# Sparse attention's scores with the queries' low parts on half of the array's rows, and six tiles of the merge's linear part computed beside it

## The chip, the cores and the metric

The kernel runs on one core of a Trainium2 chip. That core has TensorE (PE, with its weight loads shown apart as PEld), VectorE (DVE), ScalarE (ACT), GpSimd (POOL), and SyncE (SP), which here only issues transfers. The metric is the device time of one execution in microseconds, lower is better.

## The reference

A decoder layer on 1024 tokens of width 1024 in float32. It has two token mixers, native sparse attention and gated linear attention (GLA), a gated merge of the two, an output projection and a gated feed-forward part. The change touches the scores of two of the three attention branches:

```python
q_pos = lax.dynamic_slice_in_dim(q_rot, s, Q_BLOCK, axis=3) * scale          # 128 queries, head size 64
ss = jnp.einsum('bghqd,bgqnld->bghqnl', q_pos, ks, preferred_element_type=jnp.float32)   # selected blocks
p_s = masked_softmax(ss, m_s)
sw = jnp.einsum('bghqd,bgkd->bghqk', q_pos, kwin, preferred_element_type=jnp.float32)    # window of 512
p_w = masked_softmax(sw, m_w)
return gt[..., 0:1] * o_c + gt[..., 1:2] * o_s + gt[..., 2:3] * o_w
```

and where one product of the merge is computed (`merged = gate_a * (o_a @ w_up_nsa) + gate_b * (o_b @ w_up_gla)`): the GLA half, `o_b @ w_up_gla`, does not depend on the attention.

## The kernel before

**Precision.** TensorE multiplies float32 operands here as `fp32r`, which keeps a shortened mantissa. So nearly every operand is split into a high and a low part (`hi = x` rounded by ACT, `lo = x - hi` by DVE or POOL), and a product is three matmuls: hi·hi, hi·lo, lo·hi.

**Scores.** A head has 64 dimensions, the array 128 rows. The key tile `ks[br][g]` (`key_job`, `br` 0 for selected blocks and 1 for the window, `g` the key group) holds the keys' high part on the 64 rows of its group and the low part on the other 64. The query tile `qs[par]` (`unit`, one per group g and block i of 128 queries) holds in slot 0 the queries' high part on both halves of the rows, in slot 1 their low part on both halves. So one matmul of 128 rows with slot 0 (L1055 in `products`) gives hi·hi + hi·lo, and a second one with slot 1 (L1056) gives lo·hi and also lo·lo. Small bf16 matmuls of 128 columns add the masks: `mdb` on the diagonal block (L1060), `meb` on the window's far block (L1058).

**Groups of scores.** A unit (g, i) covers four heads, as pairs j = 0, 1 with heads `par` 0 and 1. For branch 1 (selected) the row of scores has w = 128·(i+1) columns, for branch 2 (window) at most 640. Up to 512 columns, `pair_scores` does both heads of a pair as one group. Beyond that, `head_scores` does one head as a group, in two parts of at most 512 columns. Over 2 key groups, 8 blocks and 2 pairs this makes 32 pair groups and 64 head groups, 96 in all. After the scores of a group DVE takes the maximum, ACT the exponential, and `weigh` multiplies by gate/sum; then PE transposes the weights (L1133), ACT and DVE split them (`pth`, `ptl`), and PE multiplies by the values (L1142).

**What sets the order on PE.** PE's order is the program's order. In the attention stage the class `Plan` writes it: it keeps a clock of its own with a cost for each step, and when no step of the attention is ready soon it takes a matmul from a queue of filler work (`fill`): gate products of the merge (`gate_job`, tiles `hh`, `hl`), and at the end the products `up_job` (tiles `obh`, `obl`), which are the GLA half of the merge for the last NU = 4 of 8 output tiles; their results go to memory (`ud`) and are read back in the merge. What the plan has not used is run in one piece when it ends (`fill.flush`). The merge (`merge_job`) then does 48 matmuls for an output tile that still needs both halves and 24 for one whose GLA half is done. The orders of the other engines come from a scheduler that works on priorities and on the free buffers of each pool.

**Buffers.** The pool tag "c" (`big`) has NBIG = 18 buffers of 4 KB a partition, for keys, queries, value tiles and many others; a new tile waits until one is free. The GLA state `st` and the zero-padded queries `QZ` have tiles of their own in the pool `mcst`.

**A step that is not changed but matters below.** `gla_diag` (L826) multiplies, for each of 8 chunks, `d["k"][r, j, :]` by `d["q"][r, j, :]` with r the rows 0 to 63 and then 64 to 127, into two different banks. It is the only step before the change in which products use one half of the rows and then the other.

Of the kernel before, what the change touches and what calls it, by code (L numbers as in the profile page):

```python
# [10 lines left out]
F32 = mybir.dt.float32  # L11
F32R = mybir.dt.float32r
BF = mybir.dt.bfloat16
U8 = mybir.dt.uint8
AF = mybir.ActivationFunctionType
OP = mybir.AluOpType
# [82 lines left out]

PAIR, PMAX, PREP = 4, 3, 3  # L100
LAT, WAIT, LOADED = 155.0, 300.0, 1500.0
NBIG, NMID, NSMALL = 18, 10, 8
SCRATCH = 2048
NU, FINE, NGATE = 4, 3, 2


class Plan:
# [52 lines left out]
    def score(self):  # L160
        b, fn, n = self.scores.popleft()
        fn()
        w = 64 if b.br == 0 else 128 * b.nkb
        if b.br == 0:
            cost = 540.0
        else:
            cost = n * (2 * max(107.0, w / 2.4) + 55.0 * (1 + (b.br == 2 and b.i >= 4)))
        self.t += cost
        self.s.pop(0)
        pf = self.p.pop(0) if b.br else 0.0  # L170
        m = n if b.br else 4
# [68 lines left out]
def layer_kernel(ctx, tc, a, outT):  # L240
    nc = tc.nc
    V, S, P, PE, SP = nc.vector, nc.scalar, nc.gpsimd, nc.tensor, nc.sync
    cst = ctx.enter_context(tc.tile_pool(name="cst", bufs=1))

    edge = ctx.enter_context(tc.tile_pool(name="edge", bufs=1, side="right"))
# [4 lines left out]
    mcst = tc.alloc_tile_pool(name="mcst", bufs=1)  # L250
# [14 lines left out]
    def bank(tag, n=512):  # L265
        return banks["pool"].tile([128, n], F32, name=tag, bufs=banks["tags"][tag])
# [30 lines left out]
    def mid(nm, dt=F32, shape=(512,)):  # L297
        return cur["pool"].tile([128, *shape], dt, name=nm, tag=cur["tag"], bufs=cur["bufs"])
# [96 lines left out]
    def products(getw, bank, xh, xl, w0, evac, fine=False):  # L395

        st, out, n = {}, [], len(xh)

        def at(k, i):
            if k + i == 0:  # L400
                st["p"] = bank()
            wh, wl = getw(w0 + k)
            w, x = ((wh, xh[k]), (wh, xl[k]), (wl, xh[k]))[i]
            PE.matmul(st["p"], w, x, start=k + i == 0, stop=k == n - 1 and i == 2)  # L404
            if k == n - 1 and i == 2:
                evac(st["p"])
# [127 lines left out]
    dst = [x[hf][:, i, :] for x, i in ((qg, 0), (qg, 1), (kg, 0)) for hf in range(2)]  # L534
# [121 lines left out]
    swap = list(range(32))  # L656
    for i in range(8):
        swap[i], swap[8 + i] = 8 + i, i
    ks = [[None, None], [None, None]]

    def key_job(br):
        def evac(p, hf):
            if hf == 0:
                ks[br] = [big(f"ks{br}{g}", F32R) for g in range(NG)]
            rc, rs = mid("rc"), mid("rs")
            SP.dma_start(rc, a["rope"][:, 0, hs(hf)])
            SP.dma_start(rs, a["rope"][:, 1, hs(hf)])
            kt, sw = mid("krt"), mid("ksw")
            scaled(kt, p, hf)
            V.stream_shuffle(sw, kt, swap)  # L670
            V.tensor_mul(kt, kt, rc)
            V.tensor_mul(sw, sw, rs)
            V.tensor_add(kt, kt, sw)
            for g in range(NG):
                r, o = slice(64 * g, 64 * g + 64), slice(64 - 64 * g, 128 - 64 * g)
                k = ks[br][g]
                S.activation(k[r, hs(hf)], kt[r, :], AF.Copy)
                V.tensor_tensor(k[o, hs(hf)], kt[r, :], f(k[r, hs(hf)]), OP.subtract)
        return a["w_t"][6 + br], proj(evac)

# [75 lines left out]
        log_sigmoid(lsg[p].rearrange("p a b -> p (a b)"), z)  # L756


    st = [[mcst.tile([128, 256], F32, name=f"st{i}{j}") for j in range(2)] for i in range(2)]
    for i in range(2):  # L760
        for j in range(2):
            P.memset(st[i][j], 0.0)
    obd = dr.tile([128, GH, T], F32, name="obd")
    ob2 = dr.tile([128, GH, T], F32, name="ob2")
    CH = {}

    QZ = [mcst.tile([128, 2, 2, 128], F32, name=f"qz{i}") for i in range(2)]
    for t in QZ:
        P.memset(t, 0.0)

    def gla_prep(c):
        d = CH[c] = {}
# [187 lines left out]
    for n, (h, hf) in enumerate(pieces):  # L960
# [4 lines left out]
        ps = ps_t()  # L965
# [4 lines left out]
        t = tz[:, 0, :]  # L970
# [15 lines left out]
    UN = {}  # L986
# [22 lines left out]
    class Branch:  # L1009
# [34 lines left out]
            if self.i == 0:  # L1044
                V.tensor_mul(p, p, cmul[:, None, :].to_broadcast([128, 4, 64]))

        def products(self, par, s, w, parts):
            d = UN[self.g, self.i]
            kk = ks[self.br - 1][self.g]
            edge = self.br == 2 and self.i >= 4  # L1050
            for o, n in parts:
                dst = s[:, o:o + n]
                kv = kk[:, 128 * self.k0 + o:128 * self.k0 + o + n]
                end = o + n == w
                PE.matmul(dst, d["qs"][par][:, 0, self.j, :], kv, start=True, stop=False)  # L1055
                PE.matmul(dst, d["qs"][par][:, 1, self.j, :], kv, start=False, stop=not end and not (edge and o == 0))  # L1056
                if edge and o == 0:
                    PE.matmul(s[:, 0:128], identb, meb, start=False, stop=not end)  # L1058
                if end:
                    PE.matmul(s[:, w - 128:w], identb, mdb, start=False, stop=True)  # L1060

        def weigh(self, pars, ps, z):

            n = len(pars)
            r, h = tiny("rr", 2, 6)[:, :n], 2 * self.j + pars[0]
            V.reciprocal(r, z[:, :n])
            V.tensor_mul(r, r, UN[self.g, self.i]["gt"][:, self.br, h:h + n])
            for i, par in enumerate(pars):
                p = self.p[par] = ps[i]
                if par:  # L1070
                    S.activation(p, p, AF.Copy, scale=r[:, i:i + 1])
                else:
                    V.tensor_scalar(p, p, r[:, i:i + 1], None, op0=OP.mult)

        def pair_scores(self):

            w = 128 * self.nkb
            s = ps_s().rearrange("p (h n) -> p h n", h=2)[:, :, :w]
            for par in range(2):
                self.products(par, s[:, par, :], w, [(0, w)])  # L1080
            nm, z = tiny("nm", 2, 6), tiny("z", 2, 6)
            V.tensor_reduce(nm, s, AX, OP.max, negate=True)
            p = prob("p", shape=(2, 512))[:, :, :w]
            for par in range(2):
                S.activation(p[:, par, :], s[:, par, :], AF.Exp, bias=nm[:, par:par + 1],
                             accum_out=z[:, par:par + 1])
            self.weigh((0, 1), [p[:, 0, :], p[:, 1, :]], z)

        def head_scores(self, par):
            w = 128 * self.nkb  # L1090
            c = w if w <= 512 else 128 * ((self.nkb + 1) // 2)
            s = ps_s()[:, 512 - c:512 - c + w]
            self.products(par, s, w, [(0, c), (c, w - c)][:1 if c == w else 2])
            nm, z = tiny("nm", 2, 6)[:, :1], tiny("z", 2, 6)[:, :1]
            V.tensor_reduce(nm, s, AX, OP.max, negate=True)
            p = prob("p")[:, :w]
            S.activation(p, s, AF.Exp, bias=nm, accum_out=z)
            self.weigh((par,), [p], z)
# [512 lines left out]
    ready, ps = deque(), {}  # L1611
# [25 lines left out]
    with tc.manual_schedule(engines={mybir.EngineType.SP}):  # L1637
# [6 lines left out]
        for i, (n, p, *h) in enumerate(todo):  # L1644
# [93 lines left out]
```

## Time and profile before

| | us |
|---|---|
| median of three timed runs (1650.31 to 1654.77) | 1653.8 |
| the profiled execution | 1651.47 |
| its span, first to last instruction | 1649.6 |
| PE busy | 1583.9 (96%) |
| DVE busy | 1070.0 (65%) |
| ACT busy | 809.7 (49%) |
| POOL busy | 752.0 (46%) |
| mean granted TensorE clock | 0.99 |

The span is 1.9 us shorter than the execution's time, and that time is 2.3 us below the median of the timed runs. In the trace the attention stage runs from about 395 us (first scores at 396.8) to 812 us (last product with values), the rest of the filler to 819, the merge to 886. A matmul's row in the timeline gives its start and a modelled length that overlaps the next one's, so what a matmul costs on a full PE is the distance from its start to the next start. If its weights were not yet loaded when it started, its row is longer by that time. A PEld row is the load of the stationary operand; "64\*128" in a row is the array area used, 64 rows by 128 columns.

### The profile page before, as it was taken

How to read it: one execution, taken by the hardware profiler on the slowest of the kernel's cores; microseconds unless marked ns; L12 is line 12 of the kernel's file. 1: busy time of each engine (PE TensorE's matmuls, PEld its weight loads, DVE VectorE, ACT ScalarE, POOL GpSimd, SP SyncE). 2: the span in 40 equal slices, each digit the busy share in tenths (PEclk: the TensorE clock that was granted, in tenths of full speed). 3: DMA queues.
4: the chain of work that ended last, by engine and by line, in shares of the span. 5: the costliest groups of instructions: out<-in, count | busy, mean ns of one | idle time of the engine just before them, and what ended most of it. 6: DMA issues, size and time to landing. Idle time of an engine off the chain costs nothing.

```text
span 1649.6 us, 23202 instructions
## 1 busy us (share of the span) xinstructions
PE 1583.9 (96%) x8079; PEld 1314.8 (80%) x8079; DVE 1070.0 (65%) x1759; ACT 809.7 (49%) x1633; POOL 752.0 (46%) x668
## 2 busy tenths in 40 slices
PE   9899999998999999998898989999999999999997
PEld 6788978876888878886777778888888888888886
DVE  7771487695777787778655476744444444489776
ACT  6231466543676666767644344433334333444542
POOL 6210376664234442345124450356665666545560
PEclk9999999999999999999999999999999999999999
DMA  5331212342111111113256551333332333595414
GB/s 175 116 105 46 72 61 74 114 140 74 43 45 43 58 46 42 45 43 103 85 175 212 195 170 45 102 101 108 119 102 97 101 103 102 209 378 153 142 47 144
DMA packets 107208, 178.82 MB, mean 108 GB/s; under 512 B 11969, under 2 KB 26706, under 8 KB 107090
## 3 DMA queue, kind: packets, MB, share of 16 engines
q1 hardware_dynamic: 103778, 171.30, 31.7%
q10 hardware_dynamic: 3312, 6.03, 1.0%
q8 instruction: 64, 1.05, 0.3%
q14 instruction: 54, 0.44, 0.1%
HBM read 129.84 MB, written 47.45 MB: 107 GB/s over the span
## 4 chain that ended last, share of the span: by engine, by line
PE 75%; DVE 9%; DMA 5%; issue 4%; ACT 4%; POOL 3%; SPq 0%; DVEq 0%; ACTq 0%; POOLq 0%
PE m L404 11%; PE m L1352 9%; PE m L1353 9%; PE d L404 9%; PE m L1354 9%; PE m L1667 4%; PE m L1668 4%; PE m L1669 4%; PE t L1133 3%; PE o L1142 3%; PE s L1055 2%; PE s L1056 2%; POOL wl L354 1%; DMA wf<-in_w_out 1%; DVE qs L1004 1%
## 5 line engine op out<-in xcount | busy, mean ns | idle before, releaser
L354 POOL TENSOR_TENSOR wl<-wf,wh 128x512 fp32r<-128x512 f32 x106 | 145.6, 1375 | 319.0 <-ACT wh L353 297.8
L1352 PE MATMUL m<-xt,wh 128*128 128x512 f32 x412 | 161.4, 392 | 2.6 <-ACT sc L1358 2.6
L1354 PE MATMUL m<-xt,wl 128*128 128x512 f32 x412 | 160.3, 389 | 0.0
L1353 PE MATMUL m<-xt,wh 128*128 128x512 f32 x412 | 160.3, 389 | 0.0
L1284 POOL TENSOR_TENSOR wl<-ws,wh 128x512 fp32r<-128x512 f32 x76 | 107.4, 1418 | 91.0 <-ACT wh L1283 71.6
L1111 DVE TENSOR_TENSOR ptl<-t,pth 128x512 fp32r<-128x512 f32 (+1 forms) x168 | 99.5, 597 | 47.4 <-ACT pth L1110 46.0
L1284 POOL TENSOR_TENSOR wl<-wr,wh 128x512 fp32r<-128x512 f32 x69 | 92.4, 1339 | 57.9 <-ACT wh L1283 56.9
L353 ACT ACTIVATE wh<-wf 128x512 fp32r<-128x512 f32 x106 | 66.4, 628 | 98.7 <-PE m L404 38.9
L1283 ACT ACTIVATE wh<-wr 128x512 fp32r<-128x512 f32 x87 | 54.9, 631 | 120.4 <-POOL wl L1284 84.0
L404 PE MATMUL m<-hh,wh 128*128 128x512 f32 x240 | 103.8, 433 | 10.0 <-DVE qr L524 5.3
L1284 POOL TENSOR_TENSOR wl<-wd,wh 128x512 fp32r<-128x512 f32 x56 | 82.4, 1474 | 61.5 <-ACT wh L1283 58.0
L1667 PE MATMUL m<-xb,wh 128*128 128x512 f32 x280 | 109.3, 390 | 0.0
L1669 PE MATMUL m<-xb,wl 128*128 128x512 f32 x280 | 108.9, 389 | 0.0
L1668 PE MATMUL m<-xb,wh 128*128 128x512 f32 x280 | 108.9, 389 | 0.0
L1110 ACT ACTIVATE pth<-t 128x512 fp32r<-128x512 f32 (+1 forms) x168 | 87.6, 526 | 38.4 <-PE t L1133 35.3
L1284 DVE TENSOR_TENSOR xb<-ar,xb 128x512 fp32r<-128x512 f32 (+1 forms) x84 | 81.3, 984 | 35.2 <-ACT xb L1283 35.2
L1283 ACT ACTIVATE wh<-ws 128x512 fp32r<-128x512 f32 x76 | 47.9, 630 | 111.9 <-PE m L1353 95.2
L404 PE MATMUL m<-hh,wl 128*128 128x512 f32 x240 | 95.8, 399 | 1.1 <-POOL wl L354 1.1
L404 PE MATMUL m<-hl,wh 128*128 128x512 f32 x240 | 95.8, 399 | 0.0
L1352 PEld LDWEIGHTS m<-xt,wh 128*128 128x128 f32 x412 | 77.3, 188 | 22.2 <-ACT sc L1358 6.4
L1133 PE MATMUL t<-ident,p 128*128 128x128 f32 x528 | 83.6, 275 | 11.2 <-DVE ptl L1111 10.0
L1354 PEld LDWEIGHTS m<-xt,wl 128*128 128x128 f32 x412 | 77.3, 188 | 16.2
(381 smaller groups left out, 4674.1 us busy)
## 6 DMA issues: line engine op xcount, KB each, us to landing
ar<-actd SPq DMA_DIRECT2D x70, 256.0 KB, 3.0
wf<-in_w_t SPq DMA_DIRECT2D x58, 256.0 KB, 2.8
wr<-in_w_gate SPq DMA_DIRECT2D x44, 256.0 KB, 2.6
wr<-in_w_upf SPq DMA_DIRECT2D x44, 256.0 KB, 2.7
zd<-zt SPq DMA_DIRECT2D x40, 256.0 KB, 2.0
wd<-in_w_down SPq DMA_DIRECT2D x33, 256.0 KB, 5.2
wf<-in_w_out SPq DMA_DIRECT2D x32, 256.0 KB, 3.2
actd<-t SPq DMA_DIRECT2D x30, 256.0 KB, 2.5
```

The source lines that it names most:

```text
L354: (eng or V).tensor_tensor(wl, wf, f(wh), OP.subtract)
L404: PE.matmul(st["p"], w, x, start=k + i == 0, stop=k == n - 1 and i == 2)
L1111: V.tensor_tensor(tl[:, :c], pt[:, :c], f(th[:, :c]), OP.subtract)
L1133: PE.transpose(pt[:, bs(2 * b + par)], self.p[par][:, bs(kb + b)], ident)
L1283: S.activation(th, src, AF.Copy)
L1284: eng.tensor_tensor(tl, src, f(th), OP.subtract)
L1352: PE.matmul(ps, wh[:, c], xh, start=first and k == 0, stop=False, skip_group_check=not first)
L1353: PE.matmul(ps, wh[:, c], xl, start=False, stop=False, skip_group_check=not first)
L1354: PE.matmul(ps, wl[:, c], xh, start=False, stop=k == MH - 1, skip_group_check=not first)
L1667: PE.matmul(dst, wh[:, c], xh, start=first and p == 0, stop=False, skip_group_check=not first)
L1668: PE.matmul(dst, wh[:, c], xl, start=False, stop=False, skip_group_check=not first)
L1669: PE.matmul(dst, wl[:, c], xh, start=False, stop=p == NP - 1, skip_group_check=not first)
```

## The change

1. **Scores.** `products` becomes `high` and `low`. `high` is the old first matmul and the masks. `low` is the second matmul on 64 rows only: it multiplies the queries' low part by the keys' high part, and no longer by the keys' low part. Its `half` argument chooses rows 0 to 63 or 64 to 127. A pair's two heads, or a head's two parts of columns, take one half each, one right behind the other, into different banks. Heads' parts are now always split evenly in blocks of 128.
2. **Keys.** A tile `kx[br]` holds each group's high keys on the rows where `ks[br][g]` has low ones; ACT writes it with 8 more copies.
3. **`weigh`.** Head 0's weight is multiplied by 1/sum and gate in one DVE instruction with two factors; the multiplication of 1/sum by the gate stays for head 1, which now goes first.
4. **Fillers.** NU goes from 4 to 6: two more `up_job` tiles (48 matmuls) move from the merge to the filler queue.
5. **The plan's costs** for a group of scores follow item 1: the two low products count as the longer of them.
6. **Buffers.** `st` and `QZ` become tiles of tag "c", whose buffers go from 18 to 20; with the two `kx` that is four more tiles for two more buffers.

```diff
-NBIG, NMID, NSMALL = 18, 10, 8
+NBIG, NMID, NSMALL = 20, 10, 8
-NU, FINE, NGATE = 4, 3, 2
+NU, FINE, NGATE = 6, 3, 2
...
-            cost = n * (2 * max(107.0, w / 2.4) + 55.0 * (1 + (b.br == 2 and b.i >= 4)))
+            c = w if n == 2 else 128 * ((b.nkb + 1) // 2)
+            cost = n * (w / 2.4 + 55.0 * (1 + (b.br == 2 and b.i >= 4))) + max(107.0, c / 2.4)
...
                 S.activation(k[r, hs(hf)], kt[r, :], AF.Copy)
+                S.activation(kx[br][o, hs(hf)], kt[r, :], AF.Copy)
...
-    st = [[mcst.tile([128, 256], F32, name=f"st{i}{j}") for j in range(2)] for i in range(2)]
+    sts = big("st", shape=(2, 2, 256))
...
-    QZ = [mcst.tile([128, 2, 2, 128], F32, name=f"qz{i}") for i in range(2)]
+    qzs = big("qz", shape=(2, 2, 2, 128))
...
-                PE.matmul(dst, d["qs"][par][:, 0, self.j, :], kv, start=True, stop=False)
-                PE.matmul(dst, d["qs"][par][:, 1, self.j, :], kv, start=False, stop=not end and not (edge and o == 0))
+        def low(self, half, par, dst, o, n):
+
+            r, br = slice(64 * half, 64 * half + 64), self.br - 1
+            kk = ks[br][self.g] if half == self.g else kx[br]
+            PE.matmul(dst, UN[self.g, self.i]["qs"][par][r, 1, self.j, :],
+                      kk[r, 128 * self.k0 + o:128 * self.k0 + o + n], start=False, stop=True)
...
-            V.tensor_mul(r, r, UN[self.g, self.i]["gt"][:, self.br, h:h + n])
...
-                    V.tensor_scalar(p, p, r[:, i:i + 1], None, op0=OP.mult)
+                    V.tensor_scalar(p, p, ri, gi, op0=OP.mult, op1=OP.mult)
...
-                self.products(par, s[:, par, :], w, [(0, w)])
+                self.high(par, s[:, par, :], w, [(0, w)])
+            for par in range(2):
+                self.low(par, par, s[:, par, :], 0, w)
...
-            self.products(par, s, w, [(0, c), (c, w - c)][:1 if c == w else 2])
+            parts = (0, c), (c, w - c)
+            self.high(par, s, w, parts)
+            for half, (o, n) in enumerate(parts):
+                self.low(half, par, s[:, o:o + n], o, n)
```

On PE, a head group of the window (group 0, block 7, w = 640) stands like this in the order before. `ks_925` is the window's key tile of group 0, `identb` the identity for the masks, `d` the bank of the filler products:

```order
L404 MATMUL d<-hl,wh 128x512
L1055 MATMUL s<-ks_925,qs 128x384
L1056 MATMUL s<-ks_925,qs 128x384
L1058 LDWEIGHTS identb
L1058 MATMUL s<-meb,identb 128x128
L1055 MATMUL s<-ks_925,qs 128x256
L1056 MATMUL s<-ks_925,qs 128x256
L1060 LDWEIGHTS identb
L1060 MATMUL s<-mdb,identb 128x128
L404 MATMUL d<-hh,wl 128x512
```

The same group in the order of the change, where `ks_930` is the same key tile and `kx_932` the new one:

```order
L405 MATMUL d<-hh,wl 128x512
L1054 MATMUL s<-ks_930,qs 128x384
L1057 LDWEIGHTS identb
L1057 MATMUL s<-meb,identb 128x128
L1054 MATMUL s<-ks_930,qs 128x256
L1059 LDWEIGHTS identb
L1059 MATMUL s<-mdb,identb 128x128
L1065 MATMUL s<-ks_930,qs 128x384
L1065 MATMUL s<-kx_932,qs 128x256
L405 MATMUL d<-hh,wh 128x512
```

Both L1065 products, of 64 rows, now stand at the end of the group, between a mask and the next product of 128 rows. The count of matmuls is the same. Of the `up_job` products, 67 stand inside the plan before and 67 after; 29 stood behind its end, now 77.

On ACT, at the start of the GLA stage, the order before has the first chunk's decay differences (`xx`) ahead of the gates' exponential (`gz`) and the last value tile (`vs`):

```order
L461 ACTIVATE lsg<-lsg 128x512
L798 ACTIVATE xx<-xx 128x1024
L799 ACTIVATE xx<-xx 128x1024
L724 ACTIVATE vs_1049<-t,rtok 128x4x64
L798 ACTIVATE xx<-xx 128x768
L799 ACTIVATE xx<-xx 128x768
L882 ACTIVATE gz<-gz 128x192
```

In the change they come behind:

```order
L462 ACTIVATE lsg<-lsg 128x512
L727 ACTIVATE vs_1058<-t,rtok 128x4x64 x2
L727 ACTIVATE vs_1059<-t,rtok 128x4x64
L884 ACTIVATE gz<-gz 128x192
L800 ACTIVATE xx<-xx 128x1024
L727 ACTIVATE vs_1059<-t,rtok 128x4x64
L801 ACTIVATE xx<-xx 128x1024
L800 ACTIVATE xx<-xx 128x768
L801 ACTIVATE xx<-xx 128x768
```

The `xx` tiles are of tag "c"; the first of them now waits for a buffer that PE's token products release.

## Rows read from the trace of the kernel before

**Rows 1.** The page's lines for the engines' busy time and for the chain of work that ended last.

```profile
PE 1583.9 (96%) x8079; PEld 1314.8 (80%) x8079; DVE 1070.0 (65%) x1759; ACT 809.7 (49%) x1633; POOL 752.0 (46%) x668
PE 75%; DVE 9%; DMA 5%; issue 4%; ACT 4%; POOL 3%; SPq 0%; DVEq 0%; ACTq 0%; POOLq 0%
```

**Rows 2.** Busy time by stretch: attention without its end, its end with the flushed fillers, the merge. Columns: stretch, length, busy us (and instructions) of PE, PEld, DVE, ACT, POOL, then granted clock, DMA share, GB/s.

```profile
395.00:750.00 355.00, 347.04 (x2176) 294.10 (x2175) 264.56 (x626) 238.58 (x575) 139.48 (x146) 1.00 0.14 48
750.00:821.00 71.00, 58.97 (x358) 49.70 (x358) 53.62 (x117) 48.09 (x134) 23.73 (x24) 0.95 0.24 81
821.00:886.00 65.00, 63.57 (x280) 52.02 (x279) 36.03 (x47) 32.00 (x55) 22.99 (x18) 1.00 0.61 197
```

**Rows 3.** What PE waited for from 395 to 815 us, the five largest: total us, times, longest.

```profile
PE t L1133 <- DVE ptl L1111: 10.0, 9, 3.0
PE d L404 <- DVE obl L1194: 3.5, 2, 2.6
PE o L1125 <- DVE oa L1157: 2.0, 2, 1.1
PE o L1125 <- DVE ptl L1111: 1.6, 1, 1.6
PE t L1133 <- DVE rr L1066: 0.9, 1, 0.9
```

**Rows 4.** The low products' groups by shape, from the view that groups PE's instructions by line and form: count, busy us, mean ns.

```profile
L1056 PE MATMUL s<-ks,qs 128*128 128x384 f32 x80 | 27.3, 341 | 0.0
L1056 PE MATMUL s<-ks,qs 128*128 128x256 f32 x56 | 15.6, 279 | 0.0
L1056 PE MATMUL s<-ks,qs 128*128 128x512 f32 x40 | 15.7, 393 | 0.0
L1056 PE MATMUL s<-ks,qs 128*128 128x128 f32 x16 | 4.5, 282 | 0.0
```

**Rows 5.** PE's timeline in two head groups of scores, one of 512 + 512 columns and one of 384 + 256: start, modelled length, line, operands.

```profile
412.67 0.39 PE L1056 MATMUL s<-ks,qs 128*128 128x512 f32 x1
412.90 0.23 PE L1060 MATMUL s<-mdb,identb 128*128 128x128 bf16 x1
...
413.25 0.40 PE L1056 MATMUL s<-ks,qs 128*128 128x512 f32 x1
...
422.33 0.34 PE L1056 MATMUL s<-ks,qs 128*128 128x384 f32 x1
422.51 0.23 PE L1058 MATMUL s<-meb,identb 128*128 128x128 bf16 x1
...
422.75 0.28 PE L1056 MATMUL s<-ks,qs 128*128 128x256 f32 x1
422.88 0.23 PE L1060 MATMUL s<-mdb,identb 128*128 128x128 bf16 x1
```

**Rows 6.** PEld's timeline around `gla_diag` of one chunk, where products of 128 rows, then 64, then 128 follow each other.

```profile
209.38 0.19 PEld L404 LDWEIGHTS m<-hh,wl 128*128 128x128 f32 x1
209.93 0.52 PEld L826 LDWEIGHTS t<-qg,kg 64*128 64x128 f32 x8 [0.36 <-issue]
210.57 0.19 PEld L404 LDWEIGHTS m<-hh,wh 128*128 128x128 f32 x1
210.68 0.19 PEld L404 LDWEIGHTS m<-hl,wh 128*128 128x128 f32 x1
```

**Rows 7.** PE's timeline at the same place.

```profile
209.37 0.39 PE L404 MATMUL m<-hl,wh 128*128 128x512 f32 x1
209.60 0.40 PE L404 MATMUL m<-hh,wl 128*128 128x512 f32 x1
209.93 0.71 PE L826 MATMUL t<-qg,kg 64*128 64x128 f32 x8
210.57 0.50 PE L404 MATMUL m<-hh,wh 128*128 128x512 f32 x1
210.91 0.39 PE L404 MATMUL m<-hl,wh 128*128 128x512 f32 x1
```

**Rows 8.** The view of line L826 alone: the products' durations (minimum, median, maximum, ns).

```profile
L826 PE MATMUL t<-qg,kg x64: 272/272/373, 198.2 to 307.6; 64*128 64x128 f32 x64
```

**Rows 9.** PE's timeline around another chunk's `gla_diag`, whose predecessor is a row of four products of 128 columns (L838).

```profile
227.00 0.61 PE L838 MATMUL t<-xq,xx 128*128 128x128 f32 x4
227.53 0.71 PE L826 MATMUL t<-qg,kg 64*128 64x128 f32 x8
```

**Rows 10.** Timelines of POOL, ACT and PE at the first GLA chunk: the decay differences' first batch, the gates' exponential, the first level's products.

```profile
192.25 2.58 POOL L796 TENSOR_TENSOR xx<-cum 128x256 f32<-128x256 f32 x4 [13.48 <-ACT cum L779]
196.20 1.94 POOL L796 TENSOR_TENSOR xx<-cum 128x256 f32<-128x256 f32 x3 [1.37 <-PE t L701]
...
195.95 1.06 ACT L799 ACTIVATE xx<-xx 128x1024 f32<-128x1024 f32 x1
200.20 0.36 ACT L882 ACTIVATE gz<-gz 128x192 f32<-128x192 f32 x1 [0.31 <-DVE gz L720]
...
200.38 1.09 PE L838 MATMUL t<-xq,xx 128*128 128x128 f32 x8
```

**Rows 11.** The view of line L677, ACT's copies of the keys' high part.

```profile
L677 ACT ACTIVATE ks<-krt x8: 627/630/632, 82.2 to 128.1; 64x512 fp32r<-64x512 f32 x8
```

More of the change, by code (lines that the diff above doesn't have):

```diff
@@ L658, in layer_kernel @@
         swap[i], swap[8 + i] = 8 + i, i
-    ks = [[None, None], [None, None]]
+    ks, kx = [[None, None], [None, None]], [None, None]
     def key_job(br):
@@ L664, in evac @@
                 ks[br] = [big(f"ks{br}{g}", F32R) for g in range(NG)]
+                kx[br] = big(f"kx{br}", F32R)
             rc, rs = mid("rc"), mid("rs")
@@ L756, in decay @@
         log_sigmoid(lsg[p].rearrange("p a b -> p (a b)"), z)
-    st = [[mcst.tile([128, 256], F32, name=f"st{i}{j}") for j in range(2)] for i in range(2)]
-    for i in range(2):
-        for j in range(2):
-            P.memset(st[i][j], 0.0)
+    sts = big("st", shape=(2, 2, 256))
+    P.memset(sts, 0.0)
+    st = [[sts[:, i, j, :] for j in range(2)] for i in range(2)]
     obd = dr.tile([128, GH, T], F32, name="obd")
@@ L765, in layer_kernel @@
     CH = {}
-    QZ = [mcst.tile([128, 2, 2, 128], F32, name=f"qz{i}") for i in range(2)]
-    for t in QZ:
-        P.memset(t, 0.0)
+    qzs = big("qz", shape=(2, 2, 2, 128))
+    P.memset(qzs, 0.0)
+    QZ = [qzs[:, i] for i in range(2)]
     def gla_prep(c):
@@ L1045, in cmp_scores, with high @@
                 V.tensor_mul(p, p, cmul[:, None, :].to_broadcast([128, 4, 64]))
-        def products(self, par, s, w, parts):
+        def high(self, par, s, w, parts):
             d = UN[self.g, self.i]
             kk = ks[self.br - 1][self.g]
-            edge = self.br == 2 and self.i >= 4
             for o, n in parts:
-                dst = s[:, o:o + n]
-                kv = kk[:, 128 * self.k0 + o:128 * self.k0 + o + n]
-                end = o + n == w
-                PE.matmul(dst, d["qs"][par][:, 0, self.j, :], kv, start=True, stop=False)
-                PE.matmul(dst, d["qs"][par][:, 1, self.j, :], kv, start=False, stop=not end and not (edge and o == 0))
[L1057 to L1060, printed above, removed]
+                PE.matmul(s[:, o:o + n], d["qs"][par][:, 0, self.j, :], kk[:, 128 * self.k0 + o:128 * self.k0 + o + n],
+                          start=True, stop=False)
+                if self.br == 2 and self.i >= 4 and o == 0:
+                    PE.matmul(s[:, 0:128], identb, meb, start=False, stop=False)
+                if o + n == w:
+                    PE.matmul(s[:, w - 128:w], identb, mdb, start=False, stop=False)
+        def low(self, half, par, dst, o, n):
[3 more added lines that the diff above has]
+                      kk[r, 128 * self.k0 + o:128 * self.k0 + o + n], start=False, stop=True)
         def weigh(self, pars, ps, z):
@@ L1066, in weigh @@
             V.reciprocal(r, z[:, :n])
-            V.tensor_mul(r, r, UN[self.g, self.i]["gt"][:, self.br, h:h + n])
-            for i, par in enumerate(pars):
-                p = self.p[par] = ps[i]
+            for i, par in reversed(list(enumerate(pars))):
+                p, ri, gi = ps[i], r[:, i:i + 1], UN[self.g, self.i]["gt"][:, self.br, h + i:h + i + 1]
+                self.p[par] = p
                 if par:
-                    S.activation(p, p, AF.Copy, scale=r[:, i:i + 1])
+                    V.tensor_mul(ri, ri, gi)
+                    S.activation(p, p, AF.Copy, scale=ri)
                 else:
-                    V.tensor_scalar(p, p, r[:, i:i + 1], None, op0=OP.mult)
+                    V.tensor_scalar(p, p, ri, gi, op0=OP.mult, op1=OP.mult)
         def pair_scores(self):
@@ L1090, in head_scores @@
             w = 128 * self.nkb
-            c = w if w <= 512 else 128 * ((self.nkb + 1) // 2)
+            c = 128 * ((self.nkb + 1) // 2)
             s = ps_s()[:, 512 - c:512 - c + w]
-            self.products(par, s, w, [(0, c), (c, w - c)][:1 if c == w else 2])
+            parts = (0, c), (c, w - c)
+            self.high(par, s, w, parts)
+            for half, (o, n) in enumerate(parts):
+                self.low(half, par, s[:, o:o + n], o, n)
             nm, z = tiny("nm", 2, 6)[:, :1], tiny("z", 2, 6)[:, :1]
```

## The prediction

> **What bounds the kernel now.** I read the page first, then the stretches, then PE's waits, then single matmuls. PE is busy 96% of the span, and 75% of the chain that ended last is PE's own work [rows 1]. By stretches, PE is busy 347.0 of 355 us in the attention up to 750, 59.0 of 71 us in its end, and 63.6 of 65 us in the merge, where DVE has 264.6, 53.6 and 36.0 us [rows 2]. So what the change adds to PE's work or takes from it moves the end almost in full. The exception is where PE waits anyway: the five largest waits from 395 to 815 us add up to 18.0 us, 14.5 of them for DVE's steps behind PE's own products and 3.5 for the loading of `obl` [rows 3].
>
> **The low products.** Before, 192 of them run on the whole array: 40 of 512 columns, 80 of 384, 56 of 256, 16 of 128 [rows 4]. On a full PE one of 512 columns costs 0.23 us (412.67 to 412.90), one of 384 costs 0.18 (422.33 to 422.51), one of 256 costs 0.13 (422.75 to 422.88) [rows 5]; for 128 I take 0.12, since with the weights' load a short product costs hardly less than one of 256. Sum 9.2 + 14.4 + 7.3 + 1.9 = 32.8 us, and this goes away.
>
> In their place stand 96 pairs of 64-row products. If the two run side by side a pair costs its longer product. By the groups' widths that is 24 pairs of 512 columns, 56 of 384, 8 of 256, 8 of 128: 24·0.23 + 56·0.18 + 8·0.13 + 8·0.06 = 17.1 us (0.06 is a quarter of 0.23; the loads are counted next). By this alone the change would save 15.7 us.
>
> **The change of the array's rows.** Each group now goes from 128 rows to 64 and back, which the trace of before shows at `gla_diag`. Going in: the last product of 128 rows starts at 209.60 and would be followed at 209.83, as its like are every 0.23 us; but the load of the 64-row weights starts only at 209.93 [rows 6, 7]. After a product of 128 columns (the last of L838's four starts 0.34 us behind the first, at 227.34, by its length of 0.27) it starts at 227.53, 0.19 later [rows 8, 9]. The load hides behind nothing: the first 64-row product is 0.10 us longer than the median one (373 against 272 ns) [rows 8]. Going out: the eight products run in 0.71 us, so the last starts 0.27 before their end, at 210.37. The next load of 128 rows starts at 210.57, 0.20 later, and is not hidden either: the product after it has 0.34 us to its successor at 210.91 where 0.23 is usual [rows 6, 7]. Elsewhere a load runs while the product before it streams.
>
> The price of a group, from its last mask to the next product's stream: 0.20 (to the low weights' load) + 0.10 (load) + the stream of the pair, counted above + 0.14 (0.20 less the 0.06 of a stream of 128 columns) + 0.11 (load) = 0.55 us. The mask's own way to the next stream is paid today too: mask at 412.90, next stream at 413.25 − 0.23 = 413.02, so 0.12 [rows 5]. That leaves 0.43 us, and 96 groups make 41.3 us. By the entry after a long product (0.33 − 0.23 + 0.06 = 0.16 in place of 0.20) it would be 37.4 us, and with 0.03 for the rounding of the four differences 44.2.
>
> So PE's work in the attention changes by −32.8 + 17.1 + 41.3 = **+25.4 us** (bounds 21.5 to 28.3). The masks and high products keep their number and neighbours.
>
> The Trainium skill says the same of the entry and the exit: its page "TensorEngine Tiling (Array Packing)", section "Tiling Modes", states that changing the tiling mode, and not merely the tile, drains TensorE. The trace agrees, with the 0.10 and 0.14 us above; the page gives no price, and the sum here goes by the rows.
>
> **What the waits absorb.** PE's waits for `ptl`, `oa` and `rr` (14.5 us [rows 3]) end when DVE is done with something PE started earlier. With each group 0.26 us longer on PE, DVE catches up, and a wait with a group or more between its cause and its end shrinks. Not at all is one end, all 14.5 us the other. I take 7, the middle, since the waits come singly and the order of the plan around them hardly changes. The `obl` waits stay: they hang on a transfer.
>
> **GLA's first chunk.** The first `xx` tile now waits for a buffer that PE's token products release; the second one does so today and starts at 196.20 instead of following the first (192.25 + 2.58) [rows 10]. ACT then does its part behind `gz` (200.20 + 0.36), 1.06 of `abs`, 0.46 of a value tile and 1.06 of `exp` (order in the change): done at about 203.1. Before it was done at 197.01 [rows 10]. DVE's product needs some 0.6 us more, so the first level, which PE starts at 200.38, can start at about 203.7. That is 3.3 us of waiting, and later waits in the same stage may give part of it back: +3 us, between 0 and 4.5.
>
> **The rest.** The 8 copies to `kx` cost ACT 0.63 us each [rows 11] and stand between the two copies DVE waits for, so PE may see a bank 0.6 us late once or twice: +0.5, between 0 and 1.5. The two extra `up_job` tiles are 48 matmuls of 0.23 us, 11 us that leave the merge and join the attention stage. They stand behind the plan's end (77 there, 29 before), so they fill no wait, and both places are full on PE: 0, and ±1 if the merge, with less PE work for the same transfers (DMA share 0.61 [rows 2]), runs into one. `weigh` spares DVE 32 small multiplications of its 53.6 and 264.6 us: 0, hidden behind PE; without that cover a gain inside the waits counted above. The plan's cheaper costs move fillers by a few places: 0, ±1.
>
> **Sum.** 1651.5 (the profiled execution) + 25.4 − 7 + 3 + 0.5 = 1673.4. The median of the timed runs is 2.3 us above the profiled one, so 1675.7; I say **1676 us**, slower by 1.3%.
>
> **The rivals.**
> - *Full price and not side by side.* The eight products at `gla_diag` need 0.11 us from pair to pair, which is as much as two streams of 0.06 in a row. So the rows don't exclude that the two halves stream one after the other. Then the other 96 products come on top, 16 of 512 columns, 24 of 384, 48 of 256 and 8 of 128: 16·0.23 + 24·0.18 + 48·0.13 + 8·0.06 = 14.7 us. 1690 us. For it: only starts and modelled lengths are seen. Against it: loads and products of the halves are recorded together.
> - *The slack takes most.* All 14.5 us of waits vanish and the GLA stage recovers: 25.4 − 14.5 + 0.5, so 1665 us; with the `obl` and smaller waits too, 1660. For it: about five groups, 1.3 us, lie between two waits of 1 us. Against it: DVE and ACT wait for PE in turn.
> - *The change of rows is free* (the other side). In the attention stage a load of 64 rows is pulled ahead of the products as other loads are, and the price of 41.3 us falls away: 25.4 − 41.3 = −15.9; PE's waits grow by about a third of that, and GLA's 3 us stay: 1653.8 − 15.9 + 5 + 3 = 1646 us, between 1640 and 1650. It decides below 0.16 us a group (15.7 us over 96): there the scores are a gain. For it: those 64-row products are plain float32 and the new ones `fp32r`. Against it: neighbours of both kinds in 128 rows show no such gap, and the gaps at `gla_diag` have no wait of that length behind them.
>
> The Trainium skill's page "TensorE: Matmul & The Clock Gate", section "Part 3: Packing small matmuls", gives the time of a pack of tiles as one matmul's plus about 4 ns for each further tile; by that alone the last rival would hold, and no run so far shows such a pack among products of 128 rows at that price.
>
> **How the numbers follow.** Forecast 1676 at 0.80, its own range 1664 to 1686 from the bounds of its terms; not side by side 0.07 (1690); slack 0.08 (1660 to 1665); free change 0.05. The range to hold 8 in 10 is 1663 to 1687. A measurement of this kernel tells 0.3% (5 us, 1649 to 1659) from no change. Faster than that comes from the free change: 0.04. Within it come the rest of that case, and a slack that goes further than its price: 0.04. Slower: 0.92.
>
> **What would show it.** In the changed kernel's PEld timeline, the loads of L1065 start together about 0.2 us after the last mask, and the next load of 128 rows about 0.14 us after the pair's stream. If they stand right behind one another, the third rival holds. From one group's last mask to the next stream there should be 0.55 us plus 0.23, 0.18, 0.13 or 0.06; twice the stream would be the first rival. PE's waits for `ptl` shrink from 11.6 us to about 5. The first L838 comes at about 204 instead of 200.4. The merge is about 11 us shorter and what is flushed ahead of it 11 us longer. My prediction fails if the price of a group is not 0.43, or if the waits give back nearly all or nothing.

## The result and the profile after

| | before | after | ratio, 95% interval |
|---|---|---|---|
| first comparison, median us (4 runs each) | 1653.88 | 1667.34 | 1.0087, 1.0058 to 1.0116 |
| repeated as a_again (4 and 11 runs) | 1650.50 | 1668.04 | 1.0107, 1.0092 to 1.0122 |

The change is slower by 13.5 to 17.5 us, about 1%. The prediction said 1676, slower by 1.3%, and its range held the time. The profiled execution of after took 1674.0 us and was the slowest of its four; that of a_again, the same kernel, took 1668.7 and is close to the median. So the stages below are read from a_again, and after stands beside it where the two differ.

| stage, us from the traces | before | after | a_again |
|---|---|---|---|
| first instruction to the first `gla_diag` | 198.22 | 197.22 | 197.70 |
| GLA and the queries, to the first attention product | 192.44 | 194.68 | 194.20 |
| attention, to the last value product of the plan | 421.66 | 434.86 | 431.83 |
| flushed fillers | 6.83 | 17.72 | 17.69 |
| merge | 67.27 | 57.32 | 56.81 |
| output projection, to the first gate product | 101.74 | 109.16 | 107.90 |
| all behind it (span less the above) | 661.4 | 661.2 | 660.7 |

From before to a_again that is −0.5, +1.8, +10.2, +10.9, −10.5, +6.2, −0.8, by the spans 17.2 us in all. Attention pays most, GLA a little, and the output projection pays 6 us which the prediction did not have. The two profiles of the new kernel agree in GLA; in attention they differ by 3.0 us, all of it in its last 63 to 65 us, where the granted clock (a mean over its two levels: 0.50 is 1.2 GHz, 1.00 is 2.4 GHz) is 0.87 in after and 0.95 in a_again.

The page of after has more PE work and nearly the same chain as [rows 1]:

```profile
PE 1606.0 (96%) x8079; PEld 1316.1 (79%) x8079; DVE 1059.9 (63%) x1723; ACT 817.9 (49%) x1645; POOL 755.6 (45%) x668
PE 77%; DVE 9%; DMA 4%; ACT 4%; issue 4%; POOL 2%; SPq 0%; DVEq 0%; ACTq 0%; POOLq 0%
```

PE's timeline of a_again in the two head groups of 512 + 512 columns whose start [rows 5] shows in before (start, modelled length, line, operands):

```profile
414.09 0.71 PE L1054 MATMUL s<-ks,qs 128*128 128x512 f32 x2
414.64 0.23 PE L1059 MATMUL s<-mdb,identb 128*128 128x128 bf16 x1
414.80 0.49 PE L1065 MATMUL s<-ks,qs 64*128 64x512 f32 x1
414.80 0.50 PE L1065 MATMUL s<-kx,qs 64*128 64x512 f32 x1
415.23 0.73 PE L1054 MATMUL s<-ks,qs 128*128 128x512 f32 x2
415.81 0.23 PE L1059 MATMUL s<-mdb,identb 128*128 128x128 bf16 x1
415.97 0.49 PE L1065 MATMUL s<-ks,qs 64*128 64x512 f32 x1
415.97 0.49 PE L1065 MATMUL s<-kx,qs 64*128 64x512 f32 x1
416.39 0.51 PE L1154 MATMUL o<-pth,vs 128*128 128x256 f32 x2
416.73 0.40 PE L1154 MATMUL o<-ptl,vs 128*128 128x256 f32 x2
```

The loads in between, from PEld's timeline:

```profile
414.64 0.10 PEld L1059 LDWEIGHTS <-identb 128*128 128x128 bf16 x1 [0.28 <-issue]
414.80 0.18 PEld L1065 LDWEIGHTS s<-ks,qs 64*128 64x128 f32 x1
414.80 0.18 PEld L1065 LDWEIGHTS s<-kx,qs 64*128 64x128 f32 x1
415.23 0.30 PEld L1054 LDWEIGHTS s<-ks,qs 128*128 128x128 f32 x2 [0.25 <-ACT pth L1122]
```

Read three distances. From the mask to the low products it is 0.16 us. The pair starts together, and from its start to the next load of 128 rows it is 0.43. That load is exposed: the two value products behind the second pair take 0.34 us (416.39 to 416.73) where two of 256 columns take 0.23. Over the 96 groups of after the median of the first distance is 0.16; that of the second is 0.43, 0.37, 0.31 and 0.255 for pairs whose longer product has 512, 384, 256 and 128 columns; and a product of 512 columns behind the pair has 0.34 to its successor where 0.23 is usual. Without its stream a change of rows therefore takes 0.16 + 0.20 + 0.11 = 0.47 us, of which a mask pays 0.12 anyway. About **0.35 us a group** is left, where the prediction had 0.43.

PE's waits of a_again from 396 to 826 us (total, times, longest), to compare with [rows 3]:

```profile
PE t L1145 <- DVE ptl L1123: 7.7, 6, 3.3
PE d L405 <- DVE obl L1206: 2.3, 2, 1.3
PE o L1137 <- DVE ptl L1123: 1.5, 1, 1.5
PE o L1137 <- DVE oa L1169: 0.7, 1, 0.7
```

The waits for `ptl` shrink from 11.6 to 9.2 us, those for `oa` and `rr` from 2.9 to 0.7, those for `obl` from 3.5 to 2.3.

### The profile page after: what moved, and what is told of

The parts are those of the page before. It is cut to its first block, busy times and chain, and to the rows that moved or that the text cites. A ratio compares the mean times of both kernels' runs of the same rounds, so it can differ in the third digit from the quotient of the medians.

```text
span 1672.2 us, 23188 instructions
## 1 busy us (share of the span) xinstructions
PE 1606.0 (96%) x8079; PEld 1316.1 (79%) x8079; DVE 1059.9 (63%) x1723; ACT 817.9 (49%) x1645; POOL 755.6 (45%) x668
## 4 chain that ended last, share of the span: by engine, by line
PE 77%; DVE 9%; DMA 4%; ACT 4%; issue 4%; POOL 2%; SPq 0%; DVEq 0%; ACTq 0%; POOLq 0%
PE d L405 10%; PE m L1364 9%; PE m L405 9%; PE m L1365 9%; PE m L1366 8%; PE o L1154 4%; PE m L1679 4%; PE m L1681 4%; PE m L1680 4%; PE t L1145 3%; PE s L1054 2%; PE s L1065 2%; PE t L703 1%; PE t L704 1%; PE t L705 1%
```

## The experiments

**a_again**: the changed kernel once more.

> The changed kernel once more, for a second profile. Theory: from the first to the last transposed tile of the attention it is 13 us longer than before, of that 96 groups of score products at about +0.2 us each (18.9 us) less some 6 us of waits that shrink; the 8.3 us that the first profile has between the plan's end and the first gate product belong to that one execution, so this profile's stretch there is within 2 us of the kernel before (176 us) and the time is about 1667. Rival: the longer flush and the merge cost 8 us every time, and the attention a matching amount less; then the stretch is about 184 us again.

1668.04 us, 1.0107 (1.0092 to 1.0122). Attention is 10.2 us longer than before, not 13. The stretch from the plan's end to the first gate product is 182.4 us against 175.9, so it is no accident of one execution. That half of the theory fell.

**b_full**: the scores undone, all else as changed.

```
-            for par in range(2):
-                self.high(par, s[:, par, :], w, [(0, w)])
-            for par in range(2):
-                self.low(par, par, s[:, par, :], 0, w)
+            for par in range(2):
+                self.products(par, s[:, par, :], w, [(0, w)])
```

(In `head_scores` and in the plan's cost likewise.)

> The changed kernel with the scores' products as before, on all 128 rows (the low ones too) and with the plan's old cost for them; buffers, copies to kx (now unread), weigh and six tiles stay. Theory: the scores' 13 us go, and what is left over before is the wait in GLA's first chunk, 2 to 3 us: 1655 to 1657. Rival (the loss lies in buffers, fillers and merge): 1661 or more.

1659.19 us, 1.0047 (1.0031 to 1.0063): between theory and rival, so something besides the scores costs some 8 us. GLA has no wait here: `kx` is unread, so its buffers come free at once, and the first level starts 2.16 us behind the first `gla_diag`, as before (a_again: 4.11). POOL's timeline of b_full shows the first `xx` tile on time:

```profile
191.23 2.57 POOL L797 TENSOR_TENSOR xx<-cum 128x256 f32<-128x256 f32 x4 [17.35 <-ACT cum L780]
195.18 1.94 POOL L797 TENSOR_TENSOR xx<-cum 128x256 f32<-128x256 f32 x3 [1.38 <-PE t L703]
```

In a_again, where `kx` is read later and keeps its buffers, the first tile waits for the token products and the second follows at once:

```profile
195.86 4.12 POOL L798 TENSOR_TENSOR xx<-cum 128x256 f32<-128x256 f32 x7 [17.16 <-issue]
```

**c_nu4**: four tiles instead of six.

```
-NU, FINE, NGATE = 6, 3, 2
+NU, FINE, NGATE = 4, 3, 2
```

> The changed kernel with four tiles beside the merge instead of six. Theory: both places are full on PE, so nothing moves: 1667, within 2 us of the changed kernel, with the flush about 11 us shorter and the merge about 11 us longer. Rival (the two extra tiles cost the merge its time for the transfers): 1659 to 1661.

1663.19 us, 1.0078 (1.0066 to 1.0091), 4.9 us below a_again: between theory and rival. The flush is 6.84 us and the merge 68.96, as expected, but the output projection takes 101.3 us instead of 107.9. There PE's waits (total, times, longest) differ, first a_again, then c_nu4, from the plan's end on:

```profile
PE m L405 <- POOL wl L355: 11.7, 11, 2.6
PE m L405 <- ACT wh L354: 3.3, 4, 1.3
```

```profile
PE m L405 <- POOL wl L355: 7.3, 8, 3.0
PE m L405 <- ACT wh L354: 2.9, 3, 1.4
```

The waits make 4.8 of the 6.6 us. The rest fits the clock: a_again runs 6.8 us of the output projection at the lower level, c_nu4 3.4, and half of the difference is 1.7, an estimate. In a_again PE had waited 1.3 us for `wh` and was waiting 2.6 for `wl` when the clock fell (view of busy time):

```profile
906.20:913.00 6.80, 5.02 (x12) 3.96 (x13) 5.95 (x6) 2.55 (x4) 2.99 (x3) 0.50 0.23 78
```

**t_batch**: the four low products of a wide unit's two heads share one change of rows.

```
-            self.high(par, s, w, parts)
-            for half, (o, n) in enumerate(parts):
-                self.low(half, par, s[:, o:o + n], o, n)
+            self.high(par, s, w, parts)
+            self.sw[par] = s
+            if not par:
+                return
+            for par in range(2):
+                for half, (o, n) in enumerate(parts):
+                    self.low(half, par, self.sw[par][:, o:o + n], o, n)
...
```

> The changed kernel, with the low products of a wide unit's two heads held back until both heads' high products and masks are done, so that four low products share one change of the array's rows: 64 changes instead of 96. Theory: a change costs 0.34 us beside its stream, so PE has 32 x 0.34 = 10.9 us less to do; DVE gets a head's scores later and has no second score buffer free meanwhile, so a part comes back as waits: 1657 to 1665. If the change itself cost nothing: 1667 or, with the waits, more. If the waits for the two heads' softmax outweigh: over 1670.

1665.09 us, 1.0094 (1.0080 to 1.0109). PE's score groups shrink by 10.4 us (118.9 to 108.5), as the price says, but attention stays at 432.2 us. The time, at the theory's upper end, is not clear of a_again's by its interval, so only the trace speaks for the price. PE's idle time in the attention grows from 13.7 to 19.8 us; the rest of the saving fits the lower clock (13.6 us at 0.50, in a_again 6.8). Both score buffers are now held at once, which may be why PE waits more; that was not tried.

**w_weigh**: the kernel before with the new `weigh` alone.

```
-            V.tensor_mul(r, r, UN[self.g, self.i]["gt"][:, self.br, h:h + n])
-            for i, par in enumerate(pars):
+            for i, par in reversed(list(enumerate(pars))):
...
+                    V.tensor_mul(ri, ri, gi)
...
+                    V.tensor_scalar(p, p, ri, gi, op0=OP.mult, op1=OP.mult)
```

> The kernel before with only weigh changed: head 1 first, the gate folded into head 0's scaling. Behind it: with the scores undone and all else as changed, the attention still took 427.6 us instead of 421.7. Theory A: weigh does it (the scaling of head 0 with two factors, a smaller product that comes later for head 1): about 1655, attention 425 to 428. Theory B: the two extra tiles' work among the attention's fillers does it: 1650 and attention within 1 us of 421.7.

1653.07 us, 1.0015 (1.0003 to 1.0027), attention 424.5 us: neither theory as it stood. `weigh` costs 2.5 us here (0.5 to 4.5 by the interval), and not 5. DVE is not busier for it (316.3 us in the attention before, 314.2 here); PE's idle time grows from 20.0 to 22.7.

**g_full_nu4**: b_full with four tiles.

> The changed kernel with the scores' products as before and with four tiles: buffers, copies to kx (unread, so their buffers come free again at once) and weigh stay. Theory A (weigh): 1654 to 1656, attention about 427, the stretch behind it 176 to 177. Theory B (six tiles): 1650 to 1651, attention 421 to 422, the stretch behind it 176.

1655.48 us, 1.0019 (1.0008 to 1.0031): a range of 1650.8 to 1659.8, of which the profiled execution is the highest (attention 428.0, granted clock 0.90 behind 751 us). By the ratio it is what `weigh` alone costs. The two tiles cost 0.28% here (b_full against this run) and 0.29% with the new scores (a_again against c_nu4): 4.6 and 4.8 us, each give or take some 3.

**v_nu4_weigh**: c_nu4 with `weigh` as before.

> The changed kernel with four tiles and with weigh as before, so that the scores and their buffers are the change alone. Theory A (weigh cost some 5 us): 1658, attention about 427. Theory B (weigh costs nothing): 1663 as with four tiles alone, attention about 432. Either way GLA's first chunk waits as in the changed kernel, 1.95 us.

1664.14 us, 1.0076 (1.0061 to 1.0091), as c_nu4 (1.0078, 1.0066 to 1.0091): theory B. With the new scores no cost of `weigh` shows, though 2 us would not either, and the scores with their buffers alone make 12.5 us (10 to 15).

**p_split**: each low product behind its own half's high products, 192 changes, none side by side.

```
             for par in range(2):
                 self.high(par, s[:, par, :], w, [(0, w)])
-            for par in range(2):
                 self.low(par, par, s[:, par, :], 0, w)
...
```

(In `head_scores` likewise.)

> The changed kernel with each half's low product right behind its own high products and mask: 192 changes of the array's rows instead of 96, and no pair side by side. Theory: a change costs 0.34 us beside its stream (0.16 from the mask to the low load, 0.20 besides the stream to the next load, 0.11 for that load, less 0.12 that a mask costs anyway), so PE has 96 x 0.34 = 32.6 us more, and 14.7 for the streams of their own: 47 us, of which waits take 5 to 12: 1703 to 1710. At the price of 0.43 that the prediction took: 56 us, 1712 to 1719. If the loss lay elsewhere and a change cost nothing: 1680.

1710.66 us, 1.0359 (1.0342 to 1.0376). That is between the ranges of the two prices, so the trace decides. PE's score groups grow from 118.9 to 165.9 us. Of these 47.0 us, 14.7 are the streams that no longer run side by side (the prediction's figure), so a change costs 32.3 / 96 = 0.34 us. Attention grows by 43.1. A low product of 512 columns alone takes as long as the pair in a_again, 0.43 us to the next product of 128 rows:

```profile
416.18 0.23 PE L1059 MATMUL s<-mdb,identb 128*128 128x128 bf16 x1
416.34 0.50 PE L1065 MATMUL s<-kx,qs 64*128 64x512 f32 x1
416.77 0.50 PE L1054 MATMUL s<-ks,qs 128*128 128x512 f32 x1
417.20 0.49 PE L1065 MATMUL s<-ks,qs 64*128 64x512 f32 x1
```

**s_serial**: both low products of a pair on the same half.

```
-                self.low(par, par, s[:, par, :], 0, w)
+                self.low(self.g, par, s[:, par, :], 0, w)
...
```

(In `head_scores` likewise.)

> The changed kernel with both low products of a pair on the same half of the rows, so that they must run one after the other (same sums, the same 96 changes of rows). Theory (in the changed kernel they do run side by side): PE has 14.7 us more to do, a third of it taken by waits: 1676 to 1683, and from the first low product to the next load of 128 rows 0.427 us becomes 0.66 for two of 512 columns. Rival (they stream in turn there too): 1668, and 0.427 stays.

1678.16 us, 1.0150 (1.0132 to 1.0169), as the theory says; PE's score groups grow by 12.7 us (118.9 to 131.6) where 14.7 were expected. From the mask to the next product of 128 rows there are now 0.82 us instead of 0.59, the 0.23 of a second stream:

```profile
412.88 0.23 PE L1059 MATMUL s<-mdb,identb 128*128 128x128 bf16 x1
413.04 0.73 PE L1065 MATMUL s<-ks,qs 64*128 64x512 f32 x2
413.70 0.73 PE L1054 MATMUL s<-ks,qs 128*128 128x512 f32 x2
```

Here `kx` is unread too, and GLA's first level again starts 2.16 us behind `gla_diag`.

**n_none**: no low products at all.

```
-            for par in range(2):
-                self.low(par, par, s[:, par, :], 0, w)
...
```

(In `head_scores` likewise; the product that is now the last one into a bank closes it.)

> The changed kernel without the low products: the scores lack the queries' low part times the keys, so no row change and no pair is left. Theory (a group pays 0.34 us for the change and its longer stream): PE has 32.6 + 17.1 = 49.7 us less than the changed kernel, and DVE's and ACT's steps come to the front in part; the waits grow by 10 to 20 us: 1628 to 1638. At the prediction's price of 0.43 it would be 58 us less on PE: 1620 to 1630. If the low products cost little of the time: 1650 or more.

1650.31 us, 0.9980 (0.9968 to 0.9991): a miss, above every theory but the last. PE's score groups shrink by 45.9 us (118.9 to 73.0), but attention by 13.8. (`kx` is unread here too, so GLA's wait is gone as well.) The other 32.1 us have two parts. PE's idle time in the attention grows by 21.4 us (13.7 to 35.0), as PE's list from 395 to 811 us shows:

```profile
PE t L1141 <- DVE ptl L1119: 12.6, 12, 3.7
PE t L1141 <- DVE rr L1072: 10.2, 6, 2.7
PE o L1133 <- DVE ptl L1119: 3.6, 1, 3.6
PE d L405 <- DVE obl L1202: 2.6, 2, 2.2
PE o L1133 <- DVE oa L1165: 2.1, 3, 1.1
```

And PE's busy time falls by 35.1 us only, 10.8 less than the groups. Behind its waits PE is granted the lower clock: seven stretches at 0.50, 27 us of this attention (two stretches, 6.8 us, in a_again), each beginning in or just behind PE's waits, 2.0 to 3.7 us of them. One stretch, in PE's timeline and in the view of busy time:

```profile
533.82 1.09 PE L1141 MATMUL t<-ident,p 128*128 128x128 f32 x4 [2.73 <-DVE rr L1072]
...
535.13 0.63 PE L405 MATMUL d<-hh,wh 128*128 128x512 f32 x1
535.56 0.63 PE L405 MATMUL d<-hl,wh 128*128 128x512 f32 x1
...
532.70:539.50 6.80, 5.68 (x19) 4.98 (x20) 3.55 (x11) 4.13 (x11) 0.00 (x0) 0.50 0.17 58
```

Products of 512 columns follow each other every 0.43 us there, where 0.23 is usual. PE is busy for 26.2 us in these stretches against 6.8 in a_again's; half of the difference, 9.7 us, is an estimate of what the clock costs. It is no accident of the traced execution: the mean granted clock of all ten executions is 0.981 to 0.986, that of all executions of the other kernels 0.985 to 0.993.

**k_nu3** and **k_nu2**: the kernel before with three and with two tiles.

```
-NU, FINE, NGATE = 4, 3, 2
+NU, FINE, NGATE = 3, 3, 2
```

> The kernel before with three tiles beside the merge instead of four. Theory from six against four tiles (1668.0 against 1663.2): a tile that is done early halves PE's work for it in the merge, while its transfers and its steps on ACT, DVE and POOL stay or grow, so the end of the merge waits; each costs 2.4 us, and 29 matmuls flushed behind the plan become 5: 1649, 2.4 us faster than before. Rival (four just hides what follows, and the attention lacks fillers at its end): 1651 to 1653.

> The kernel before with two tiles beside the merge. Theory of 2.4 us a tile: 1646.7. But 48 matmuls fewer than four tiles give stand against 29 that were left over, so the attention's end lacks 19 fillers of 0.23 us, up to 4.4 us of waits: 1647 to 1651. Rival (four hides all): 1655 or more.

Three: 1648.96 us, 0.9979 (0.9968 to 0.9990). That is where its theory put it, faster than before by 0.2%, a little less than the 0.3% that the prediction named as the limit, though the interval leaves 1 out. Its trace does not show where the gain lies: the profiled execution took 1652.4 us, nearly the slowest of its twelve. Two: 1652.12 us, 0.9992 (0.9981 to 1.0004), no change and a miss, 1 us above its theory: the plan has no filler left to flush (the merge starts 0.25 us behind its end). The output projection goes on getting shorter (100.8 and 97.8 us), the merge longer (73.0 and 77.6).

## Why the prediction was right, and by which sizes it was off

**Lows removed, −32.8.** Right: the distances behind before's 192 low products add up to 32.6 us.

**Side by side, +17.1.** Right in mechanism; the figure itself is the sum of the longer streams. The second low product starts 3 ns behind the first, a pair of 512 takes the 0.43 us that one alone takes in p_split, and in turn (s_serial) it takes 0.66. The rival "not side by side" is excluded. The Trainium skill's page "TensorE: Matmul & The Clock Gate", section "Part 3: Packing small matmuls", gives one matmul's time plus some 4 ns for each further tile; the trace agrees, with these 3 ns.

**The change of rows, +41.3: mis-sized.** Measured 33 to 34: PE's score groups take 118.9 us in a_again and 120.2 in after, against 101.3 before; 118.9 − (101.3 − 32.6) − 17.1 = 33.1, or 0.345 us a group, and p_split gives 0.34. This lies below the lower bound of 37.4, and by the prediction's own sign ("fails if the price of a group is not 0.43") this step failed. By n_none the same reckoning gives 45.9 − 17.1 = 28.8, or 0.30 a group; its rows hold 2.6 us of waits and 6.1 us at the lower clock, a_again's 1.6 and 2.8, which explains over half of the difference. Two parts were too dear. The entry is 0.16 (taken: 0.20 from behind L838 at 227.34). And the load's 0.10 and the exit's 0.14 together are 0.20 beside the stream instead of 0.24, at every width. I had read the one from a product's length and the other from a row of eight short products. The exposed load of the way out, 0.11, was right. "Free" is excluded: it asked for less than 0.16. The Trainium skill's page "TensorEngine Tiling (Array Packing)", section "Tiling Modes", states that changing the tiling mode drains TensorE; the trace agrees that a change costs, with these 0.34 to 0.35 us, and the page has no price.

**What the waits absorb, −7.** Right in size: PE's groups grow by 17.6 us and attention by 10.2, so 7.4 (in after 18.9 and 13.2, so 5.7). The place was half right, since `ptl` kept 9.2 of its 11.6 us where about 5 was expected, while `oa` and `rr` lost 2.2 of 2.9. The rival "slack takes most" is excluded.

But the statement that what is added or taken "moves the end almost in full" holds only for what is added on top of the changed kernel. The experiments make a curve (groups: distance from the first product of an unbroken row of score products to the second one behind it, summed over the 75 rows; the others from the view of busy time over the stretch):

| kernel | PE in score groups | PE busy | attention | attention less PE busy |
|---|---|---|---|---|
| n_none | 73.0 | 383.0 | 418.1 | 35.0 |
| before | 101.3 | 401.7 | 421.7 | 20.0 |
| a_again | 118.9 | 418.2 | 431.8 | 13.7 |
| s_serial | 131.6 | 430.2 | 442.8 | 12.6 |
| p_split | 165.9 | 465.0 | 475.0 | 10.0 |

Of each us more in the groups attention pays 0.13, then 0.58, 0.87 and 0.94 (with w_weigh's 424.5 in before's place, since the others have the new `weigh`: 0.23 and 0.41 for the first two). The first figure holds the lower clock too: without the 9.7 us estimated for it n_none's attention would be about 408 us, and the 0.13 about 0.5. The row of n_none, with DVE at 316 of 418 us, and the one of a_again (stretch, length, then busy PE, PEld, DVE, ACT, POOL; clock; DMA share; GB/s):

```profile
390.45:808.50 418.05, 383.02 (x2323) 321.48 (x2321) 316.43 (x712) 284.16 (x709) 161.66 (x169) 0.97 0.16 52
```

```profile
391.90:823.73 431.83, 418.15 (x2515) 338.80 (x2514) 312.20 (x712) 285.26 (x709) 161.98 (x169) 0.99 0.15 51
```

So work taken from PE in the kernel before mostly comes back: of the 28.3 us that n_none's groups are shorter, 15.0 are idle time of PE, most of it ended by DVE's `ptl` and `rr`, and about 9.7 go to the clock. What the waits would cost without the clock falling behind them was not tried. A change of rows for nothing would have won little: n_none, with neither the change nor the low streams and with the same six tiles, took 1650.3, so the rival's 1646, with a third lost to waits, was too good.

**GLA, +3.** Right as a mechanism and near in size. The first `xx` tile waits, shown by b_full and s_serial, where it doesn't and the wait is gone. The first level comes 1.95 us later against `gla_diag` (expected 3.3; ACT starts `gz` at 198.16 in a_again, not at 200.20 as assumed), the last level 2.8 us later. To the first attention product 1.8 to 2.2 is left.

**Six tiles, 0 ± 1: wrong.** Measured 4.6 and 4.8 us in two pairs of kernels, give or take some 3. The traces agree: from the plan's end to the first gate product the seven with six tiles (after included) take 179.3 to 184.2 us, the five with four 174.6 to 179.3. Flush +10.9 and merge −10.5 came as predicted; the step that failed is that no transfer or step behind them would come late. Each early tile halves PE's time for its part of the merge, while its loads, its ACT and DVE steps stay and it adds two loads of `u` and two products on POOL. At the merge's end POOL works these off among the output weights' low parts, and `m` waits for `wl`. POOL's timeline of a_again, around the first output products at 898.2:

```profile
897.77 1.68 POOL L1249 TENSOR_TENSOR zb<-u,zb 128x512 f32<-128x512 f32 x1 [2.00 <-PE m L405]
899.41 1.27 POOL L355 TENSOR_TENSOR wl<-wf,wh 128x512 fp32r<-128x512 f32 x1
901.65 1.34 POOL L1249 TENSOR_TENSOR zb<-u,zb 128x512 f32<-128x512 f32 x1 [0.97 <-DMA u<-ud]
904.99 1.27 POOL L1249 TENSOR_TENSOR zb<-u,zb 128x512 f32<-128x512 f32 x1 [2.00 <-DMA u<-ud]
906.21 1.71 POOL L355 TENSOR_TENSOR wl<-wf,wh 128x512 fp32r<-128x512 f32 x1
```

PE's side of the last of these rows, with the wait that it ends:

```profile
907.98 0.79 PE L405 MATMUL m<-mg,wl 128*128 128x512 f32 x1 [2.62 <-POOL wl L355]
```

With c_nu4 this place is shown. Whether POOL's queue or the late transfers of `u` ahead of it are the cause was only read, not tried.

**`weigh`, 0.** Right in the changed kernel as far as the runs can tell (v_nu4_weigh against c_nu4: 0.02%), not in the kernel before, where it costs 2.5 us (0.5 to 4.5). The two findings are too close to tell them apart, so that the changed kernel hides the cost is possible but not shown. Why it costs anything stays open: DVE's busy time falls by 2.1 us in w_weigh, and it is PE's waits that grow.

**Sum.** By a_again: PE +17.6, waits −7.4, GLA and queries +1.8, output projection +6.2, the rest (start, flush and merge, all behind) −0.9: +17.2 by the spans where +21.9 was predicted. (The predicted +25.4 for PE was mis-added: its terms −32.8, +17.1 and +41.3 make 25.6, its bounds 21.7 and 28.5. These 0.2 us decide nothing.) The forecast came this close partly by luck: two errors of opposite sign, −8 at the change of rows and +6 behind the plan, largely cancel.

## What to carry to other kernels

Price a change of the array's rows by itself: here about 0.35 us for each way there and back, so half-height products side by side pay only where the streams that they save between one change and the next exceed that. Where PE is 95% busy and DVE 75%, test with a kernel that leaves the work out before expecting PE's savings as time: 46 us less on PE gave 14, since PE then waited and, behind its waits, ran in part at the lower clock. Work moved ahead as filler is not free when the place it leaves also hid transfers and another engine's queue.

## What the runs showed of the hardware that was not expected

The change of rows costs the same beside its stream for 128, 256, 384 and 512 columns (0.20 us from the pair's start to the next load, less the stream), and four low products in one change (t_batch) cost only their second stream more: 0.66 us from the first to the next load for 512 columns. The exposed load in front of a product of 128 rows is 0.11 us whether one or four 64-row products came before it. Two 64-row products of 512 and 384 columns side by side take as long as two of 512 (0.428 and 0.430 us to the next load, medians of after).
